# A new list-scheduled head, and weight blocks grouped over three and two PSUM banks, in an RMSNorm and QKV projection kernel

## The chip, the cores and the metric

The kernel runs on one core of one Trainium2 chip. The metric is the device time of one execution in microseconds (us). A kernel's time is the median of its runs. Single-core runs have no second die to be compared with, so a run counts as fast unless it is over 1.5% above the fastest run of the same kernel. The mean clock that the throttle granted to TensorE is recorded for each run, and it will matter here. In the profiles PE is TensorE's matmuls and PEld its weight loads; DVE, ACT and POOL are the vector, scalar and GpSimd engines; SP is the engine that issues the transfers. "The ring" or "the rings" is the queue of transfers that SP has issued and that the DMA engines work off.

## The reference

```python
def reference(x, gamma, w_qkv, eps):
    rms = np.sqrt(np.mean(x ** 2, axis=-1, keepdims=True) + eps)
    x_norm = x / rms * gamma
    return np.matmul(x_norm, w_qkv).astype(np.float32)
```

x is 8 × 1024 × 768 in float32, which makes 8192 rows. w_qkv is 768 × 2304. The kernel takes the rows in 64 tiles of 128. A tile needs six blocks of K (768 / 128) and five pieces of N (four of 512 columns and one of 256), so it takes 24 matmuls of full width and 6 of half width.

## The kernel before

Every tile of x is loaded, cast to bf16 and transposed to xT. The blocks of xT are the weights that TensorE loads, and w_b (w_qkv times gamma, in bf16) streams past them. The sum of a tile and a piece lies in one PSUM bank; `evac` scales it by 1/rms on DVE or ACT into `ot`, and a store brings it out.

```python
def load_x(t):
    X[t] = xin.tile([P, K], f32, name="x_t")
    nc.sync.dma_start(out=X[t], in_=xf[t * P:(t + 1) * P, :])
# load_w and store are nc.sync.dma_start too
def trans_dma(t):
    XT[t] = xTp.tile([P, KO, P], bf16, name="xT")
    nc.sync.dma_start_transpose(out=XT[t], in_=XB[t])

def mm(t, n0, kos):
    nl = min(NT, N - n0)
    for ko in kos:
        ...  # takes a PSUM bank on first use
        nc.tensor.matmul(out=PM[t, n0][:, :nl], lhsT=XT[t][:, ko, :],
                         rhs=w_b[:, ko, n0:n0 + nl], start=(b == 1), stop=(b == KO))
```

All loads, stores and DMA transposes are issued from SP, in one order. `at(time, ...)` puts an operation into a list, which is sorted by the planned time before anything is issued. The times only fix the order. An operation that has to wait holds up those behind it on its engine: in the trace of the changed kernel SP issued nothing from 11.89 to 20.02 us, in front of a transpose whose input came at 19.99, and a load that needed nothing from it was issued only after that, at 21.39.

The first six tiles are the head. They run while w_qkv is still arriving, by a list of planned operations, and there TensorE itself transposes all six tiles ("tr" and "cp"). The loads are all put first:

```python
ARRIVALS = "xxxwwwxwwwwwxxwww"            # order of the loads of x tiles and w pieces
HEAD_PLAN = [ (4.41, "trA", 0), ...
    (17.24, "tr", 4), ... (18.02, "cp", 4, "DVE"), (18.23, "tr", 5), ...
    (19.86, "mm", 4, 0, "012345"), ... (22.45, "mm", 5, 0, "012345"), ... ]
HEAD_END = 44.51

US = 6 * 0.2158 / 512
now, flip = HEAD_END, 0
for t in range(HEAD, MT):
    at(now - 15, load_x, t)
    at(now - 8.5, cast, t)
    at(now - 7.5, trans_dma, t)
    ...                                     # stat, recip
    for n0 in range(0, N, NT):
        at(now, mm, t, n0, range(KO))
        now += min(NT, N - n0) * US
        flip ^= 1
        evac_at(now + 0.2, t, n0, "DVE" if flip else "ACT", gap=1.2)   # and the store after it
```

Of the kernel before, what the change touches and what calls it, by code (L numbers as in the profile page):

```python
# [7 lines left out]



ARRIVALS = "xxxwwwxwwwwwxxwww"
PIECES = [(0, 1, 0, 512), (1, 2, 0, 512), (2, 3, 0, 512), (3, 4, 0, 512), (4, 5, 0, 512), (5, 6, 0, 512), (0, 3, 512, 512), (3, 6, 512, 512), (0, 6, 1024, 512), (0, 6, 1536, 512), (0, 6, 2048, 256)]

EARLY = 3


HEAD_PLAN = [
    (4.41, "trA", 0), (4.45, "stat", 0), (5.28, "trB", 0), (5.42, "cpA", 0, "DVE"),
    (5.71, "trA", 1), (5.85, "cpB", 0, "ACT"), (6.10, "recip", 0), (6.44, "stat", 2),
    (6.59, "trB", 1), (6.73, "cpA", 1, "DVE"), (6.80, "trA", 2), (7.11, "conv", 0, 0, "POOL"),  # L20
    (7.24, "trB", 2), (7.41, "cpB", 1, "DVE"), (7.77, "cpA", 2, "ACT"),
    (7.81, "conv", 1, 1, "DVE"), (8.02, "mm", 0, 0, "0"), (8.23, "mm", 1, 0, "0"),
    (8.29, "recip", 2), (8.39, "cpB", 2, "ACT"), (8.45, "conv", 2, 2, "DVE"),
    (8.45, "mm", 2, 0, "0"), (8.66, "mm", 0, 0, "1"), (8.75, "stat", 1), (8.88, "mm", 1, 0, "1"),
    (9.10, "mm", 2, 0, "1"), (9.31, "mm", 0, 0, "2"), (9.44, "cast", 3, "DVE"),
    (9.53, "mm", 1, 0, "2"), (9.74, "mm", 2, 0, "2"), (10.05, "tr", 3), (10.08, "stat", 3),
    (10.11, "conv", 3, 3, "DVE"), (10.59, "recip", 1), (10.65, "mm", 0, 0, "3"),
    (10.78, "conv", 4, 4, "DVE"), (10.87, "mm", 1, 0, "3"), (11.09, "mm", 2, 0, "3"),
    (11.26, "cp", 3, "DVE"), (11.32, "mm", 0, 0, "4"), (11.45, "conv", 5, 5, "ACT"),
    (11.54, "mm", 1, 0, "4"), (11.76, "mm", 2, 0, "4"), (11.82, "recip", 3),  # L30
    (11.97, "mm", 3, 0, "01234"), (13.05, "mm", 0, 0, "5"), (13.27, "mm", 1, 0, "5"),
    (13.47, "conv", 6, 0, "DVE"), (13.47, "conv", 6, 1, "ACT"), (13.47, "conv", 6, 2, "POOL"),
    (13.48, "mm", 2, 0, "5"), (13.70, "mm", 3, 0, "5"), (13.95, "evac", 2, 0, "DVE"),
    (14.01, "mm", 0, 512, "0"), (14.18, "evac", 0, 0, "ACT"), (14.22, "mm", 1, 512, "0"),
    (14.44, "mm", 0, 512, "12"), (14.70, "evac", 1, 0, "DVE"), (14.87, "evac", 3, 0, "ACT"),
    (14.87, "mm", 1, 512, "12"), (15.30, "mm", 2, 512, "012"), (15.48, "conv", 7, 4, "DVE"),
    (15.48, "conv", 7, 5, "POOL"), (15.95, "mm", 3, 512, "012"), (16.33, "conv", 7, 3, "POOL"),
    (16.47, "cast", 4, "DVE"), (16.47, "stat", 4), (16.60, "mm", 0, 512, "45"),
    (17.03, "mm", 1, 512, "4"), (17.24, "tr", 4), (17.47, "cast", 5, "DVE"),
    (17.58, "mm", 0, 512, "3"), (17.79, "mm", 1, 512, "35"), (17.80, "stat", 5),  # L40
    (18.02, "cp", 4, "DVE"), (18.23, "tr", 5), (18.56, "mm", 2, 512, "345"), (18.58, "recip", 4),
    (18.74, "evac", 1, 512, "DVE"), (19.13, "evac", 0, 512, "ACT"), (19.21, "mm", 3, 512, "345"),
    (19.49, "evac", 2, 512, "DVE"), (19.86, "mm", 4, 0, "012345"), (20.02, "evac", 3, 512, "ACT"),
    (20.24, "recip", 5), (20.40, "cp", 5, "DVE"), (21.15, "mm", 4, 512, "012345"),
    (21.49, "conv", 8, 2, "DVE"), (21.49, "conv", 8, 3, "ACT"), (21.97, "conv", 8, 0, "DVE"),
    (22.20, "conv", 8, 4, "ACT"), (22.45, "mm", 5, 0, "012345"), (22.45, "evac", 4, 0, "DVE"),
    (22.91, "evac", 4, 512, "ACT"), (23.60, "conv", 8, 1, "ACT"), (23.74, "mm", 5, 512, "012345"),
    (23.90, "evac", 5, 0, "DVE"), (24.31, "conv", 8, 5, "ACT"), (25.04, "mm", 0, 1024, "012345"),
    (25.20, "evac", 5, 512, "DVE"), (25.51, "conv", 9, 0, "POOL"), (25.51, "conv", 9, 1, "ACT"),
    (25.95, "conv", 9, 5, "DVE"), (26.33, "mm", 1, 1024, "012345"), (26.43, "conv", 9, 4, "DVE"),  # L50
    (26.49, "evac", 0, 1024, "ACT"), (26.91, "conv", 9, 2, "DVE"), (27.39, "conv", 9, 3, "DVE"),
    (27.63, "mm", 2, 1024, "012345"), (27.87, "evac", 1, 1024, "DVE"),
    (27.90, "conv", 10, 0, "POOL"), (27.90, "conv", 10, 2, "ACT"), (28.38, "conv", 10, 3, "ACT"),
    (28.62, "conv", 10, 5, "DVE"), (28.86, "conv", 10, 4, "ACT"), (28.92, "conv", 10, 1, "DVE"),
    (28.92, "mm", 3, 1024, "012345"), (29.22, "evac", 2, 1024, "DVE"),
    (30.22, "mm", 4, 1024, "012345"), (30.38, "evac", 3, 1024, "DVE"),
    (31.51, "mm", 5, 1024, "012345"), (31.67, "evac", 4, 1024, "DVE"),
    (32.81, "mm", 0, 1536, "012345"), (32.97, "evac", 5, 1024, "DVE"),
    (34.10, "mm", 1, 1536, "012345"), (34.26, "evac", 0, 1536, "DVE"),
    (35.39, "mm", 2, 1536, "012345"), (35.55, "evac", 1, 1536, "DVE"),  # L60
    (36.69, "mm", 3, 1536, "012345"), (36.85, "evac", 2, 1536, "DVE"),
    (37.98, "mm", 4, 1536, "012345"), (38.14, "evac", 3, 1536, "DVE"),
    (39.28, "mm", 5, 1536, "012345"), (39.44, "evac", 4, 1536, "DVE"),
    (40.57, "mm", 0, 2048, "012345"), (40.73, "evac", 5, 1536, "DVE"),
    (41.23, "mm", 1, 2048, "012345"), (41.39, "evac", 0, 2048, "ACT"),
    (41.88, "mm", 2, 2048, "012345"), (42.04, "evac", 1, 2048, "DVE"),
    (42.54, "mm", 3, 2048, "012345"), (42.70, "evac", 2, 2048, "DVE"),
    (43.19, "mm", 4, 2048, "012345"), (43.35, "evac", 3, 2048, "DVE"),
    (43.85, "mm", 5, 2048, "012345"), (44.01, "evac", 4, 2048, "DVE"),
    (44.67, "evac", 5, 2048, "DVE"),  # L70
]
HEAD_END = 44.51


@with_exitstack
def kernel(
# [8 lines left out]
    nc = tc.nc  # L85
    f32 = mybir.dt.float32
# [7 lines left out]
    Kw, N = w_qkv.shape  # L94
    assert K == Kw
    P = 128
    KO = K // P
    MT = M // P
    NT = 512
    HEAD = ARRIVALS.count("x")  # L100
    inv_k = 1.0 / float(K)
    PIECE_BUFS = {(k1 - k0, n): sum((q[1] - q[0], q[3]) == (k1 - k0, n) for q in PIECES)
                  for k0, k1, _, n in PIECES}

# [7 lines left out]
    xbp = ctx.enter_context(tc.tile_pool(name="xbp", bufs=4))  # L112
    xTp = ctx.enter_context(tc.tile_pool(name="xTp", bufs=HEAD + 3))
    outp = ctx.enter_context(tc.tile_pool(name="outp", bufs=7))
    psum = ctx.enter_context(tc.tile_pool(name="psum", bufs=8, space=bass.MemoryType.PSUM))
# [17 lines left out]
    w_b = singles.tile([P, KO, N], bf16)  # L133
    wv = w_qkv.rearrange("(ko p) n -> p ko n", p=P)

    X, XB, XT, RS, OUT, WF, PM, PT = {}, {}, {}, {}, {}, {}, {}, {}
# [5 lines left out]
    def load_w(c):  # L142
        k0, k1, n0, n = PIECES[c]
        WF[c] = wst.tile([P, k1 - k0, n], f32, name=f"w_f{k1 - k0}_{n}", bufs=PIECE_BUFS[k1 - k0, n])
        nc.sync.dma_start(out=WF[c], in_=wv[:, k0:k1, n0:n0 + n])  # L145

    def conv(c, ko, eng):
        k0, k1, n0, n = PIECES[c]
        o, i, g = w_b[:, ko, n0:n0 + n], WF[c][:, ko - k0, :], g_sb[:, ko:ko + 1]
# [60 lines left out]
# [3 lines that stand above are left out]
            if (t, n0) not in PM:  # L213
# [2 lines left out]
            nc.tensor.matmul(out=PM[t, n0][:, :nl], lhsT=XT[t][:, ko, :], rhs=w_b[:, ko, n0:n0 + nl],  # L216
                             start=(b == 1), stop=(b == KO))

    def part(n0):
        return max(i for i, (p0, _) in enumerate(PARTS) if p0 <= n0)  # L220

# [20 lines left out]
    def at(time, fn, *args):  # L242
        plan.append((time, len(plan), fn, args))
# [8 lines left out]
    def evac_at(time, t, n0, eng, gap):  # L252
        at(time, evac, t, n0, eng)
        h = part(n0)
        nl = min(NT, N - n0)
        left[t, h] = left.get((t, h), PARTS[h][1]) - nl
        if t == MT - 1:
            at(time + gap - 0.5, store, t, h, n0, nl)
        elif left[t, h] == 0:
            at(time + gap, store, t, h, *PARTS[h])  # L260
# [4 lines left out]
            nc.tensor.matmul(out=wps, lhsT=warm, rhs=warm, start=True, stop=True)  # L265


    nx = nw = 0
    for n, kind in enumerate(ARRIVALS):
        if kind == "x":  # L270
            at(0.1 * n - 9, load_x, nx)
            nx += 1
        else:
            at(0.1 * n - 9, load_w, nw)
            nw += 1
    at(0.0, idle, 30)
    ops = {"conv": conv, "cast": cast, "stat": stat, "recip": recip, "tr": tr, "cp": cp, "mm": mm}
    for time, op, *args in HEAD_PLAN:
# [14 lines left out]
    US = 6 * 0.2158 / 512  # L293
    now, flip = HEAD_END, 0
    for t in range(HEAD, MT):
        at(now - 15, load_x, t)
        at(now - 8.5, cast, t)
        at(now - 7.5, trans_dma, t)
        at(now - 5, stat, t)
        at(now - 3, recip, t)  # L300
        for n0 in range(0, N, NT):
            at(now, mm, t, n0, range(KO))
            now += min(NT, N - n0) * US
            flip ^= 1
            evac_at(now + 0.2, t, n0, "DVE" if flip else "ACT", gap=1.2)

    for _, _, fn, args in sorted(plan, key=lambda p: p[:2]):
        fn(*args)
# [35 lines left out]
```

## Time and profile before

| | before |
|---|---|
| time, median of 3 runs | 389.47 us (389.18 to 389.6) |
| span of the profiled run | 387.9 us |
| TensorE's share of the chain that ended last | 94% |
| first matmul of the product | 8.5 us |
| start of tile 6, the end of the head | 45.1 us |
| start of tile 7, and time of one tile from there on | 51.56 us, 5.835 us |
| granted TensorE clock | full in all slices |

The kernel is bound by TensorE; the prediction shows the lines and the sums. So there is little to gain, while a loss has no such limit.

### The profile page before, as it was taken

What the parts mean: (1) busy time and instruction counts of PE and PEld (TensorE: products, weight loads), DVE (VectorE), ACT (ScalarE), POOL (GpSimd) and SP (SyncE); (2) the same over time, 40 slices, a digit from 0 to 9 for tenths busy, and PEclk for the clock granted to TensorE, in tenths of its full rate; (3) what the DMA queues carried; (4) which work ended last, traced back from release to release, by engine and by line L of the source; (5) the groups of instructions that cost most, each with busy time, mean ns of one, the idle gap of its engine ahead of it and who ended that gap; (6) DMA issues with size and microseconds to landing.
All of it is one profiled execution on the core that took longest, in us unless ns stands there. A gap on an engine that the chain in (4) does not pass through costs nothing.

```text
span 387.9 us, 5500 instructions
## 1 busy us (share of the span) xinstructions
PE 379.5 (98%) x1953; PEld 194.3 (50%) x1992; DVE 159.1 (41%) x317; ACT 178.1 (46%) x359; POOL 5.9 (2%) x12
## 2 busy tenths in 40 slices
PE   7999999999999999999999999999999999999996
PEld 6444644554554554554554554554554554554553
DVE  3667634343433343433343433343334343334332
ACT  6652234544444544444534444534434535434532
POOL 1310000000000000000000000000000000000000
PEclk9999999999999999999999999999999999999999
DMA  7999999999999999999999999999999999999974
GB/s 272 392 384 358 308 369 284 397 301 274 333 311 305 279 326 295 290 330 300 276 346 288 302 317 280 318 311 304 287 318 301 297 318 303 287 325 292 292 264 189
DMA packets 87606, 119.51 MB, mean 308 GB/s; under 512 B 50710, under 2 KB 59676, under 8 KB 87580
## 3 DMA queue, kind: packets, MB, share of 16 engines
q1 hardware_dynamic: 87568, 119.17, 100.7%
q8 instruction: 15, 0.25, 0.3%
q14 instruction: 11, 0.09, 0.1%
q10 hardware_dynamic: 12, 0.00, 0.0%
HBM read 32.25 MB, written 75.50 MB: 278 GB/s over the span
## 4 chain that ended last, share of the span: by engine, by line
PE 94%; DMA 3%; SPq 1%; issue 1%; DVE 0%; ACT 0%
PE pm L216 94%; DMA w_f<-in_w_qkv_dram 2%; DMA xT<-xb 2%; SPq L140 0%; SPq L145 0%; PE pm L183 0%; DVE w_b L151 0%; ACT ot L232 0%; DVE ot L230 0%
## 5 line engine op out<-in xcount | busy, mean ns | idle before, releaser
L216 PE MATMUL pm<-w_b,xT 128*128 128x512 bf16 (+1 forms) x1881 | 372.4, 357 | 3.0 <-DMA xT<-xb 0.4
L216 PEld LDWEIGHTS <-xT 128*128 128x128 bf16 x1920 | 187.6, 98 | 186.6 <-issue 0.8
L230 DVE TENSOR_SCALAR ot<-pm,rstd 128x512 f32<-128x512 f32 (+1 forms) x168 | 116.7, 696 | 210.3 <-PE pm L216 210.3
L232 ACT ACTIVATE ot<-pm,rstd 128x512 f32<-128x512 f32 (+1 forms) x152 | 97.9, 645 | 187.0 <-PE pm L216 141.7
L170 ACT ACTIVATE sq<-x_t 128x768 bf16<-128x768 f32 x64 | 53.4, 834 | 10.2 <-DMA x_t<-in_x_dram 10.2
L159 DVE CAST xb<-x_t 128x768 bf16<-128x768 f32 x61 | 33.2, 545 | 4.1 <-DMA x_t<-in_x_dram 4.0
L172 ACT ACTIVATE rms<-ssq,eps_sb 128x1 f32<-128x1 f32 x64 | 18.8, 294 | 2.1
L170 ACT ACTIVATION_READ_ACCUMULATOR sq<-x_t 128x1 f32 x64 | 12.2, 191 | 0.0
L177 DVE RECIPROCAL rstd<-rms 128x1 f32<-128x1 f32 x64 | 9.8, 153 | 0.0
L151 DVE TENSOR_SCALAR w_b<-w_f,g_sb 128x512 bf16<-128x512 f32 (+1 forms) x14 | 6.5, 494 | 6.1 <-DMA w_f<-in_w_qkv_dram 6.0
L153 ACT ACTIVATE w_b<-w_f,g_sb 128x512 bf16<-128x512 f32 (+1 forms) x10 | 6.1, 651 | 5.7 <-DMA w_f<-in_w_qkv_dram 5.7
L155 POOL TENSOR_SCALAR w_b<-w_f,g_sb 128x512 bf16<-128x512 f32 (+1 forms) x6 | 5.2, 864 | 23.5 <-DMA w_f<-in_w_qkv_dram 23.5
L265 PE MATMUL pm<-warm 128*128 128x128 bf16 x35 | 3.8, 300 | 1.0 <-DVE eps_sb L124 1.0
L265 PEld LDWEIGHTS <-warm 128*128 128x128 bf16 x35 | 3.5, 142 | 1.0 <-DVE eps_sb L124 1.0
L197 PE MATMUL pm<-ident_f,x_t 128*128 128x128 f32 x18 | 2.8, 292 | 0.8 <-DMA x_t<-in_x_dram 0.8
L197 PEld LDWEIGHTS pm<-ident_f,x_t 128*128 128x128 f32 x18 | 2.2, 155 | 1.1 <-DMA x_t<-in_x_dram 1.0
L127 ACT ACT_TABLE_LOAD x1 | 1.3, 1283 | 1.3 <-PEq L325 1.3
L159 DVE CAST xT<-pm 128x512 bf16<-128x512 f32 (+1 forms) x3 | 1.7, 596 | 0.0
L159 DVE COPY xT<-pm 128x768 bf16<-128x768 bf16 x3 | 1.6, 547 | 0.0
L248 DVE COPY g_sb<-pm 128x6 f32<-128x6 f32 x1 | 0.2, 165 | 3.6 <-PE pm L247 3.6
L183 PEld LDWEIGHTS <-xb 128*128 128x128 bf16 x18 | 1.2, 98 | 0.9 <-DVE xb L159 0.6
L183 PE MATMUL pm<-ident,xb 128*128 128x128 bf16 x18 | 1.5, 220 | 0.0
(13 smaller groups left out, 3.1 us busy)
## 6 DMA issues: line engine op xcount, KB each, us to landing
out_dram<-ot SPq DMA_DIRECT2D x126, 512.0 KB, 4.0
x_t<-in_x_dram SPq DMA_DIRECT2D x64, 384.0 KB, 4.3
out_dram<-ot SPq DMA_DIRECT2D x64, 128.0 KB, 3.2
w_f<-in_w_qkv_dram SPq DMA_DIRECT2D x2, 1536.0 KB, 13.3
w_f<-in_w_qkv_dram SPq DMA_DIRECT2D x3, 768.0 KB, 8.5
w_f<-in_w_qkv_dram SPq DMA_DIRECT2D x6, 256.0 KB, 5.8
out_dram<-ot SPq DMA_DIRECT2D x4, 256.0 KB, 2.0
xT<-xb SPq DMA_TRANSPOSE x58, 4.4
```

The costliest lines, as they stand in the source:

```text
L151: nc.vector.tensor_scalar(out=o, in0=i, scalar1=g, scalar2=None, op0=mult)
L153: nc.scalar.activation(out=o, in_=i, func=AF.Copy, scale=g, bias=0.0)
L155: nc.gpsimd.tensor_scalar(out=o, in0=i, scalar1=g, scalar2=1.0, op0=mult, op1=mult)
L159: nc.vector.tensor_copy(out=out, in_=in_)
L170: nc.scalar.activation(out=sq, in_=X[t], func=AF.Square, accum_out=ssq)
L172: nc.scalar.activation(out=rms, in_=ssq, func=AF.Sqrt, scale=inv_k, bias=eps_sb)
L177: nc.vector.reciprocal(out=r, in_=RS[t])
L197: nc.tensor.transpose(out=PT[t, h][:, ko - k0, :], in_=X[t][:, ko * P:(ko + 1) * P], identity=ident_f)
L216: nc.tensor.matmul(out=PM[t, n0][:, :nl], lhsT=XT[t][:, ko, :], rhs=w_b[:, ko, n0:n0 + nl], start=(b == 1), stop=(b == KO))
L230: nc.vector.tensor_scalar(out=o, in0=pm[:, :nl], scalar1=RS[t], scalar2=None, op0=mult)
L232: nc.scalar.activation(out=o, in_=pm[:, :nl], func=AF.Copy, scale=RS[t], bias=0.0)
L265: nc.tensor.matmul(out=wps, lhsT=warm, rhs=warm, start=True, stop=True)
```

## The change

It has two parts. The loop after the head takes the pieces of N in a group of three and a group of two, goes through the six weight blocks once for each group, and marks all but the first matmul of a block as needing no weight load. In the head, a new list moves the transposes of tiles 4 and 5 from TensorE to the DMA, cuts the weight pieces smaller, and puts the last three of them (w11, w12 and w13) and the tiles x6 and x7 behind those transposes.

```diff
-ARRIVALS = "xxxwwwxwwwwwxxwww"
-PIECES = [(0, 1, 0, 512), ... , (0, 6, 2048, 256)]
+PIECES = [ ... (0, 2, 512, 512), (2, 4, 512, 512), (4, 6, 512, 512), (0, 3, 1024, 512), (3, 6,
+          1024, 512), (0, 3, 1536, 512), (3, 6, 1536, 512), (0, 6, 2048, 256)]
+LOADS = [
+    (-9.00, "x", 0), ... (-8.86, "x", 4),
+    (-8.85, "w", 10), (-8.84, "x", 5), (18.73, "t", 4), (18.74, "w", 11), (22.11, "t", 5),
+    (22.12, "w", 12), (22.13, "w", 13), (22.14, "x", 6), (22.15, "x", 7),
+]
 HEAD_PLAN = [ ...                      # all times and the order are new; no "tr" or "cp" of 4 and 5
-HEAD_END = 44.51
+HEAD_END = 43.73
...
+    def mm_shared(t, n0s):
+        for n0 in n0s:
+            PM[t, n0] = psum.tile([P, NT], f32, name="pm")
+        for ko in range(KO):
+            for n0 in n0s:
+                ...
+                if n0 == n0s[0]:
+                    m = nc.tensor.matmul(out=o, lhsT=l, rhs=r, start=(ko == 0), stop=(ko == KO - 1))
+                    lhs = m.ins.ins[1]
+                else:
+                    nc.tensor.add_instruction(mybir.InstMatmult( ...
+                        ldweights=False, ins=[nc.tensor.lower_ap(r), lhs], ...))
...
-    nx = nw = 0
-    for n, kind in enumerate(ARRIVALS):
-        ...
+    for time, kind, n in LOADS:
+        at(time, {"x": load_x, "w": load_w, "t": trans_dma}[kind], n)
...
     for t in range(HEAD, MT):
-        at(now - 15, load_x, t)
+        if ("x", t) not in {q[1:] for q in LOADS}:
+            at(now - 15, load_x, t)
...
-        for n0 in range(0, N, NT):
-            at(now, mm, t, n0, range(KO))
-            ...
+        n0s = list(range(0, N, NT))
+        groups = [[n0] for n0 in n0s] if t == MT - 1 else [n0s[:3], n0s[3:]]
+        for g in groups:
+            at(now, mm_shared, t, g)
+            now += sum(min(NT, N - n0) for n0 in g) * US
+            for j, n0 in enumerate(g):
+                flip ^= 1
+                evac_at(now + 0.2 + 0.35 * j, t, n0, "DVE" if flip else "ACT", gap=1.2)
```

## The prediction

The prediction reckons with 2.5 ns per matmul, which can be worked out from the trace of before. From 70 to 370 us matmuls of 512 columns start 215.83 ns apart in the mean and those of 256 columns 109.17 ns, so 2 × 109.17 - 215.83 = 2.5 ns of a matmul do not go with its columns. The weight loads of 98 ns run beside the matmuls there: one matmul starts at 100.198 us and a load at 100.199. The pool for the sums has eight tiles in PSUM, and the kernel issues everything on SP in one order.

> **What bounds the kernel now.** I read the page first (engine shares, the slices, the chain's shares, the costliest groups), then the tile view of xT, then the chain and the timelines piece by piece.
>
> ```profile
> span 387.9 us, 5500 instructions
> PE 379.5 (98%) x1953; PEld 194.3 (50%) x1992; DVE 159.1 (41%) x317; ACT 178.1 (46%) x359; POOL 5.9 (2%) x12
> PEclk9999999999999999999999999999999999999999
> GB/s 272 392 384 358 308 369 284 397 301 274 333 311 305 279 326 295 290 330 300 276 346 288 302 317 280 318 311 304 287 318 301 297 318 303 287 325 292 292 264 189
> ...
> PE 94%; DMA 3%; SPq 1%; issue 1%; DVE 0%; ACT 0%
> ...
> L216 PE MATMUL pm<-w_b,xT 128*128 128x512 bf16 (+1 forms) x1881 | 372.4, 357 | 3.0 <-DMA xT<-xb 0.4
> L216 PEld LDWEIGHTS <-xT 128*128 128x128 bf16 x1920 | 187.6, 98 | 186.6 <-issue 0.8
> ```
>
> TensorE is the bound: 94% of the chain is its matmuls, at full clock, and they idle 3.0 us in all. The weight loads are counted busy for 187.6 us, but on their own row beside the matmuls. What matters is whether a load delays the next matmul, and the timeline of TensorE in the steady stretch answers it:
>
> ```profile
> 99.98 3.62 PE L216 MATMUL pm<-w_b,xT 128*128 128x512 bf16 x16
> ```
>
> Sixteen matmuls of 512 columns span 3.62 us; the last is shown as 0.379 us long, so 15 starts lie in 3.24 us: 0.216 us each. [...]every one of these matmuls has a 98 ns load of its own. The load is already hidden.
>
> The tile view of xT gives the ends of the stream, and the timeline of the weight loads gives the only wait outside the head:
>
> ```profile
> L216 PE MATMUL pm<-w_b,xT x1881: 272/379/390, 8.5 to 384.1; 128*128 128x512 bf16 x147, 128*128 128x256 bf16 x42
> ...
> DMA to landing us min/median/max: 3.2/4.4/6.9
> ```
>
> ```profile
> 51.56 10.48 PEld L216 LDWEIGHTS <-xT 128*128 128x128 bf16 x53 [0.72 <-DMA xT<-xb]
> ```
>
> Tile 7 starts at 51.56. From there to about 384.17 (the last start plus 0.11) 57 tiles run, 332.6 us, 5.835 us per tile of 24 full and 6 half-width matmuls. All 64 tiles are 373.4 us of streaming. The stretch from 8.5 to 384.17 is 375.7, so only 2.3 us of it is not streaming: 0.7 for PE transposes of tiles 4 and 5, 0.3 for tile 3's, 0.6 for the wait before tile 7 (0.72 less one half-width matmul), the rest small waits for converted weights before 15 us. Outside lie 8.5 us before the first real matmul and 3.7 us after the last.
>
> Two chain pieces show the transposes' cost on the path, and one the wait:
>
> ```profile
> 17.99 0.34 PE pm L183 x6
> ...
> 19.01 0.34 PE pm L183 x6
> ...
> 45.48 6.04 DMA xT<-xb
> ```
>
> [...]every matmul here has its own load, so nothing in it says whether the 2.5 ns belongs to the matmul or to the change of weights. [...]groups of three and two need five per tile. [...]all loads, stores and transposes here are issued from SP. [...]the timeline of SP before tile 7's transpose is
>
> ```profile
> 40.43 2.26 SPq L236 DMA_DIRECT2D out_dram<-ot  x3
> 42.78 1.05 SPq L140 DMA_DIRECT2D x_t<-in_x_dram  x1
> 43.92 1.46 SPq L236 DMA_DIRECT2D out_dram<-ot  x2
> 45.48 1.39 SPq L206 DMA_TRANSPOSE xT<-xb  x1
> ```
>
> Five stores and a load lay ahead of it, and it took 6.04 us against a median of 4.4: that made the 0.6 us wait.
>
> **The change, part by part.**
>
> Part one, shared weights. For 57 tiles (6 to 62) 30 loads become 12, so 57 × 18 = 1026 loads of 98 ns vanish, 100 us of load-row time, all beside other work. On the path only the 2.5 ns can go, and only if it belongs to the load: 1026 × 2.5 ns = 2.6 us. [...]I give the saving 35 in 100, so about -0.9 as expectation. The last load of each pair group (98 ns) still hides under a half-width matmul (109 ns), as it does now.
>
> PSUM: the group of three takes 24/6 × 0.97 = 3.88 us, the group of two 1.94. The first bank of a group of two is the eighth allocated before it, in the three of the previous tile's group; there is more than 3.8 us to empty it, against 0.7 us per eviction on either engine. DVE and ACT are 41% and 46% busy, and their work is unchanged. No wait.
>
> Part two, the head. Removed: twelve PE transposes, 2 × 0.34 = 0.7 us on the path, which is nearly all of what the plan's own end promises (43.73 for 44.51). Moved: tiles 4 and 5 are transposed by DMA; three late weight pieces are issued after those transposes; x6 and x7 are loaded early, so tile 7's 0.6 us wait should go.
>
> The new order puts transfers in front of transposes. I follow the ring. Through x5 the queue holds 6 × 384 KB of x and 6 × 256 + 3 × 512 + 2 × 768 KB of weights, 7.08 MB. The slices of 9.70 us moved 2.64 and 3.80 MB, then 0.384 MB/us: reached at 19.4 + 0.64/0.384 = 21.1 us. A check of the method on the kernel before: its x5 stood at 5.50 MB, reached at 9.7 + 2.86/0.392 = 17.0, and its cast began at 18.03, so landing costs 1 us more.
>
> ```profile
> 18.03 0.56 DVE L159 CAST xb<-x_t 128x768 bf16<-128x768 f32 x1 [0.44 <-DMA x_t<-in_x_dram]
> ```
>
> After the change x4 (5.90 MB) lands near 19.0, its cast ends at 19.6, and its transpose goes into the ring behind w10 and x5; with 1 to 2 us of its own it lands near 23. Tile 4 is wanted at 24.26 by the plan, plus about 0.6, by which the kernel before ran behind its plan (tile 6 began at 51.56 - 0.6 - 5.835 = 45.1 for 44.51). That fits. Tile 5 does not: by the plan's order w11 (0.79 MB) and the first stores of tiles 0 to 3 (4 × 512 KB = 2.10 MB) are issued between the two transposes. From 22.6: w11 to 24.6; the stores, at the rate that the windows view shows where stores alone ran,
>
> ```profile
> 44.00:47.00 3.00, 2.95 (x20) 1.88 (x20) 1.83 (x4) 0.00 (x0) 0.00 (x0) 1.00 1.03 422
> ```
>
> take 5.0 us, to 29.6; the transpose lands about 31. TensorE wants tile 5 at 28.15 + 0.6 = 28.75. The estimate is a wait of 2.3 us, between 1 and 4.
>
> After that w12 lands near 33 and w13 near 35; their matmuls come at 36 and 40 plus the delay, so they fit. The six second stores are now released every 0.65 us by plan (1.3 before), 3.1 MB in front of tile 7's transpose: I expect 0.4 us of wait there, between 0 and 1.
>
> Sum: -0.7 (transposes) - 0.6 (old wait) + 2.3 (tile 5) + 0.4 (tile 7) = +1.4; with the -0.9 for shared weights +0.5. 389.47 + 0.5 = 390.0 us.
>
> **Rivals.** One: the 2.5 ns is the price of changing weights. For it: the trace has no matmul without a load to contradict it. [...]It would make 388.3 with my head (+1.4 - 2.6). Two: the transposes are not held up, because stores leave gaps that they use or the 1 to 2 us are shorter; for it: steady transposes land in 4.4 us with stores about, and from 22.7 that is 27.1, in time. Then the head gains 1.3: 388.2, or 385.6 with rival one. Three: the ring holds up more than I think (transposes that stall behind others, w11 to w13 late as well): tile 4 also waits and tile 7 again, 393. Four: matmuls that keep their weights are slower, or lose the pull-ahead of the next load and show 98 ns per group and row: 57 × 12 × 0.1 = 68 us slower. Against it: loads are issued in order just before the matmul that needs them, as now. Under 4 in 100.
>
> **Range and chances.** The path can't shrink by more than 2.3 + 2.6 us plus a little at the start, so 2% (7.8 us) faster is all but excluded; slower by 7.8 needs rival four. Rivals one and two set the low end (386.8), rival three the high end (392.4).
>
> **What would show it.** Weight loads fall to about 960 and their busy time to about 94 us. The starts of matmuls in the steady stretch stay 0.2158 apart (parts: 5.835 us per tile); 5.79 would prove rival one. The chain shows a wait for DMA xT<-xb at tile 5 around 28 to 31 us, with DMA busy on 4096-byte store packets before it; if there is none, my ring argument is wrong. Tile 6 starts at 46 to 47.5 (before 45.1). A tile period over 5.9, or evictions on the chain, would make the prediction wrong altogether.

## The result, and the profile after

Ratios here are the mean time of one kernel's fast runs over that of the kernel before in the same rounds, so they are not quite the ratio of the medians that are quoted beside them.

| | before, same rounds | after |
|---|---|---|
| median | 389.54 us (4 runs) | 395.38 us (4 runs, 393.44 to 396.94) |
| ratio, 95% interval | | 1.0148 (1.0102 to 1.0194) |
| start of tile 6 | 45.1 us | 49.89 us |
| start of tile 7 | 51.56 us | 56.63 us |
| time of one tile from there on | 5.835 us | 5.835 us |

The change is 1.5% slower, which is outside the predicted range of 386.8 to 392.4 us. The four runs differ more than those of before, and the granted clock follows them:

| run of after, us | 395.19 (profiled) | 393.44 | 396.94 | 395.58 |
|---|---|---|---|---|
| span, us | 393.1 | 391.3 | 394.8 | 393.4 |
| mean granted clock | 0.996 | 1.000 | 0.990 | 0.996 |
| span × clock, us | 391.5 | 391.3 | 390.9 | 391.8 |

Without the throttle all four spans would be about 391.4 us. So about 3.5 us are lost in every run (391.4 against before's 387.9), and 0 to 4 us more differ from run to run.

The page of the changed kernel has these lines where the prediction shows those of before. In the groups the columns are line, engine, operation, tiles, shapes, count, busy us, mean ns, and the idle time ahead of them with what ended it.

```profile
span 393.1 us, 5526 instructions
PE 383.0 (97%) x1980; PEld 194.1 (49%) x1980; DVE 159.8 (41%) x312; ACT 174.5 (44%) x357; POOL 7.9 (2%) x17
PEclk9998999999999999999999999999999999999999
...
PE 90%; DMA 8%; SPq 1%; DVE 0%; issue 0%; ACT 0%
...
L241 PE MATMUL pm<-w_b,xT 128*128 128x512 bf16 (+1 forms) x714 | 246.8, 378 | 0.7 <-DMA xT<-xb 0.7
...
L244 PEld LDWEIGHTS <-xT 128*128 128x128 bf16 x1026 | 100.4, 98 | 84.6
...
L229 PE MATMUL pm<-w_b,xT 128*128 128x512 bf16 (+1 forms) x180 | 37.4, 368 | 4.2 <-DMA xT<-xb 3.5
```

Three things stand here. First, line 244 is the matmul marked as needing no load, and yet 1,026 weight loads of 98 ns bear its name. With 714 of line 241 and 180 of line 229 there are 1,920 loads of xT, exactly as before. Sharing did not happen at all. The loads stand in the built program: an experiment below takes the repeated ones out of it, and 894 of 1,920 are left in its trace. Second, the idle time ahead of the head's matmuls (line 229) is 4.2 us, of which a transpose ended 3.5. Third, the fourth slice of the clock shows an 8.

The timeline of TensorE shows where the first wait lies (start, length, engine, line, operation and count; the idle time ahead is in brackets).

```profile
27.19 2.11 PE L229 MATMUL pm<-w_b,xT 128*128 128x512 bf16 x9
32.76 4.95 PE L229 MATMUL pm<-w_b,xT 128*128 128x512 bf16 x15 [3.47 <-DMA xT<-xb]
```

At 32.76 tile 5 begins. The last matmul ahead of it is drawn 0.38 us long, while a matmul takes 0.22 from start to start, so the delay is 3.47 + 0.38 - 0.22 = 3.63 us. The same working gives 0.90 us for tile 7, whose transpose ended a wait of 0.74 us after a half-width matmul: 0.74 + 0.27 - 0.11. The chain that ended last has both, and both times it goes through a transpose (start, length, what):

```profile
25.32 7.40 DMA xT<-xb
...
32.76 17.31 PE pm L229 x90
...
51.09 5.49 DMA xT<-xb
```

The windows view of the stretch around the first wait shows what came behind it (from and to, length, busy time of PE, PEld, DVE, ACT and POOL with counts, granted clock, DMA share, GB/s).

```profile
29.00:32.70 3.70, 0.30 (x2) 0.00 (x0) 0.75 (x1) 0.00 (x0) 0.00 (x0) 0.97 1.10 341
32.70:35.80 3.10, 3.04 (x8) 1.09 (x9) 0.26 (x1) 0.00 (x0) 0.96 (x2) 0.50 1.06 369
35.80:49.80 14.00, 14.00 (x84) 8.02 (x83) 7.77 (x15) 5.09 (x11) 2.48 (x5) 1.00 0.88 310
```

For 3.1 us after the wait TensorE ran at half clock, and then it ran at full clock again. Eight matmuls took 3.27 us instead of 1.73, so 1.55 us are lost. That is the whole throttle of this run: 0.4% of 393 us.

Why the transpose came so late is to be seen four to twelve us earlier. The timeline of SP, with nothing issued between 12 and 20 us:

```profile
20.02 1.32 SPq L219 DMA_TRANSPOSE xT<-xb  x1
21.39 0.57 SPq L158 DMA_DIRECT2D w_f<-in_w_qkv_dram  x1
22.05 3.17 SPq L268 DMA_DIRECT2D out_dram<-ot  x4
25.32 2.23 SPq L219 DMA_TRANSPOSE xT<-xb  x1
```

SP stood in front of tile 4's transpose until the cast of x4 ended at 19.99, and w11, which needed nothing from it, stood behind. Then came the four stores, and then tile 5's transpose. That is the order which the prediction had followed. What it had not seen is how little the rings moved meanwhile, here in the windows view of before and then of after:

```profile
20.00:24.00 4.00, 4.00 (x20) 1.83 (x19) 2.09 (x6) 1.53 (x4) 0.00 (x0) 1.00 1.05 387
```

```profile
20.00:24.00 4.00, 3.96 (x20) 1.70 (x18) 2.56 (x6) 2.82 (x8) 0.00 (x0) 1.00 0.91 175
```

Before moved 387 GB/s here, after moved 175. The mean busy share is nearly the same (1.05 and 0.91), but it hides two things. From 20.5 to 21.5 us and from 23 to 24 us it is 0.56 and 0.64, so there the DMA engines partly lacked work. From 21.5 to 22 us it is 2.29 (packets overlap) with only 212 GB/s, so there the packets were slow: the DMA view of these four us has 822 of 1,019 packets under 512 bytes. The experiment with w11 first, below, gives an estimate of what each is worth. The shortfall is (387 - 175) × 4 = 0.85 MB, which at 0.39 MB/us is 2.2 us of transfer pushed back.

### The profile page after: what moved, and what is told of

Its sections match the earlier page's. It is cut to its first block, busy times and chain, and to the rows that moved or that the text cites. A ratio compares the mean times of both kernels' runs of the same rounds, so it can differ in the third digit from the quotient of the medians.

```text
span 393.1 us, 5526 instructions
## 1 busy us (share of the span) xinstructions
PE 383.0 (97%) x1980; PEld 194.1 (49%) x1980; DVE 159.8 (41%) x312; ACT 174.5 (44%) x357; POOL 7.9 (2%) x17
## 4 chain that ended last, share of the span: by engine, by line
PE 90%; DMA 8%; SPq 1%; DVE 0%; issue 0%; ACT 0%
PE pm L244 46%; PE pm L241 38%; PE pm L229 5%; DMA xT<-xb 3%; DMA w_f<-in_w_qkv_dram 3%; DMA x_t<-in_x_dram 2%; SPq L158 0%; SPq L153 0%; DVE w_b L164 0%; DVE ot L262 0%; ACT ot L264 0%; SPq L268 0%; DVE rstd L190 0%; SPq L219 0%
## 5 line engine op out<-in xcount | busy, mean ns | idle before, releaser
L244 PE MATMUL pm<-w_b,xT 128*128 128x512 bf16 (+1 forms) x1026 | 296.6, 344 | 0.0
L241 PE MATMUL pm<-w_b,xT 128*128 128x512 bf16 (+1 forms) x714 | 246.8, 378 | 0.7 <-DMA xT<-xb 0.7
L264 ACT ACTIVATE ot<-pm,rstd 128x512 f32<-128x512 f32 (+1 forms) x154 | 96.4, 646 | 194.4 <-PE pm L244 93.8
L262 DVE TENSOR_SCALAR ot<-pm,rstd 128x512 f32<-128x512 f32 (+1 forms) x166 | 112.4, 693 | 145.7 <-PE pm L241 72.0
L229 PE MATMUL pm<-w_b,xT 128*128 128x512 bf16 (+1 forms) x180 | 37.4, 368 | 4.2 <-DMA xT<-xb 3.5
L172 DVE CAST xb<-x_t 128x768 bf16<-128x768 f32 x61 | 34.0, 558 | 8.9 <-DMA x_t<-in_x_dram 8.7
L166 ACT ACTIVATE w_b<-w_f,g_sb 128x512 bf16<-128x512 f32 (+1 forms) x6 | 3.8, 648 | 13.2 <-DMA w_f<-in_w_qkv_dram 13.2
L168 POOL TENSOR_SCALAR w_b<-w_f,g_sb 128x512 bf16<-128x512 f32 (+1 forms) x11 | 7.2, 663 | 30.1 <-DMA w_f<-in_w_qkv_dram 22.7
```

What stands on the lines that cost most here:

```text
L168: nc.gpsimd.tensor_scalar(out=o, in0=i, scalar1=g, scalar2=1.0, op0=mult, op1=mult)
L172: nc.vector.tensor_copy(out=out, in_=in_)
L241: m = nc.tensor.matmul(out=o, lhsT=l, rhs=r, start=(ko == 0), stop=(ko == KO - 1))
L244: nc.tensor.add_instruction(mybir.InstMatmult(name=nc.get_next_instruction_name(), engine=m.ins.engine, start_tensor_calc=(ko == 0), stop_ ...
L262: nc.vector.tensor_scalar(out=o, in0=pm[:, :nl], scalar1=RS[t], scalar2=None, op0=mult)
L264: nc.scalar.activation(out=o, in_=pm[:, :nl], func=AF.Copy, scale=RS[t], bias=0.0)
```

## The experiments

All twelve kernels gave correct results. They ran in three batches, each on a chip of its own; each batch had its own runs of the kernel before (medians 389.86, 390.16 and 389.98 us), and every kernel is compared with those of its batch. "Loss" is the kernel's median minus that of before in the same rounds. For the change itself it is 395.38 - 389.54 = 5.84 us. Differences between the losses of two batches are less sharp than those within one.

### Which half of the change costs, the grouping or the head?

**Old head, grouped loop.** The kernel before with `mm_shared` and the grouped loop.

```diff
+    def mm_shared(t, n0s): ...            # as in the change
-        for n0 in range(0, N, NT): ...
+        groups = [[n0] for n0 in n0s] if t == MT - 1 else [n0s[:3], n0s[3:]]
+        ...
```

> The head of before with the grouped loop of the change. The built program still has a weight load ahead of every matmul, so theory A (the grouping changes nothing but the order) expects the time of before, 389.5 us within 0.5, 1920 loads of xT, and a tile period of 5.835 us. Rival B (the groups of three and two cost something by themselves, through evictions or the clock) expects 391 us or more. Rival C (some loads are saved on the chip) expects 387 us.

Measured: 389.76 us (13 runs), ratio 0.9999 (0.9991 to 1.0007). Grouping by itself changes nothing. The tile view of xT shows once more that the loads are there:

```profile
L231 PEld LDWEIGHTS <-xT x1026: 97/98/99, 45.2 to 378.0; 128*128 128x128 bf16 x171
```

**New head, plain loop.** The changed kernel with the loop of before.

```diff
-        groups = ...
+        for n0 in range(0, N, NT):
+            at(now, mm, t, n0, range(KO))
+            ...
```

> The head of the change with the plain loop of before: the other half of the change. Theory A expects the whole loss here: 393.4 to 397 us, the wait for tile 5's transpose of 3 to 4 us near 29 us, and the same spread from run to run. Rival B expects less than half of the loss, under 392.

Measured: 397.47 us (4 runs, 396.08 to 398.41), ratio 1.0194 (1.0172 to 1.0216), a loss of 7.6 us. This profiled run too has half clock behind the wait for tile 5, and that wait is longer, 4.25 us against 3.63. The time lies half a us above the expected range. The whole loss is in the head. In the profiled run the plain loop even makes it larger: tile 7 waits 0.99 us here and tile 8 waits 0.78. The intervals of the two kernels overlap, so that part is not shown by the times.

### Would really sharing the weights have gained anything?

**Loads dropped.** Old head and grouped loop, and the repeated loads are taken out of the built program, with their waits moved to the matmul that follows. The edit is given in words:

```diff
+   # in the built program, for the PE instructions in order:
+   #   a Ldweights of xT with the operand of the Ldweights before it is left out;
+   #   what it waited for is put on the next Matmult
```

It sets the case that the 2.5 ns belong to the matmul (389.7 us, 5.835 us per tile) against the case that they belong to the change of weights.

> As e1_old_head_grouped, but the repeated weight loads are taken out of the built program, so that 894 loads of xT stay of 1920: what the change meant to do, with the head of before. [...]the time is that of e1, 389.7 within 0.3, and a tile takes 5.835 us. If they belong to the change of weights, 1026 times 2.5 ns go: 387.1 within 0.4, and a tile takes 5.79 us. If matmuls that keep their weights are slower or expose the next load: over 392.

Measured: 389.48 us (22 runs), ratio 0.9986 (0.9978 to 0.9995). Only line 231 of this kernel, the shared matmuls, has lost its loads. Its tile view of xT:

```profile
L231 PE MATMUL pm<-w_b,xT x1003: 272/379/379, 46.0 to 378.6; 128*128 128x512 bf16 x111, 128*128 128x256 bf16 x57
L228 PEld LDWEIGHTS <-xT x714: 96/98/98, 45.6 to 384.4; 128*128 128x128 bf16 x179
L228 PE MATMUL pm<-w_b,xT x702: 272/379/390, 45.8 to 384.5; 128*128 128x512 bf16 x174, 128*128 128x256 bf16 x2
```

Line 231 has no row of loads any more, so 714 + 180 = 894 loads are left of 1,920. Tile 7 begins at 51.98 in this run, and the last matmul at 384.5: (384.5 + 0.11 - 51.98) / 57 = 5.835 us per tile, to the nanosecond that of before. So the 2.5 ns belong to the matmul and not to the change of weights. The timing shows 0.14% less than before, in a batch whose runs of before were the highest of the three; the profile has no place where this would have been gained, and the last experiment looks at it again.

### What makes tile 5 wait, and what is the wait worth?

**First stores after x7.** In the changed kernel the first stores of tiles 0 to 3 go behind the transpose of tile 5 and what follows it.

```diff
-            at(time + gap, store, t, h, *PARTS[h])
+            at(22.16 if t < 4 and h == 0 else time + gap, store, t, h, *PARTS[h])
```

> The changed kernel, but the first stores of tiles 0 to 3 are issued after the transpose of tile 5, w12, w13, x6 and x7 instead of before them. Theory (the transpose of tile 5 waits in the ring behind w11 and 2.1 MB of stores): it lands near 27 us, the wait at tile 5 (3.6 us) and the half clock after it (1.7 us in the profiled run) go, the spread of the runs shrinks below 0.5 us, and the time is 388.5 to 390.5. Rival (the transpose is slow by itself, or its issue from SP is what comes late): a wait of over 2 us stays, 392 us or more.

Measured: 393.86 us (5 runs), ratio 1.0099 (1.0082 to 1.0116), a loss of 4.0 us. The wait for tile 5 is gone, so it needed the stores in front of that transpose. But the loss is mostly still there: a wait of 3.0 us stands at tile 7, and the clock is again 0.996 in four runs of five. The two queues of TensorE at that place:

```profile
53.99 0.10 PEld L241 LDWEIGHTS <-xT 128*128 128x128 bf16 x1 [3.25 <-DMA xT<-xb]
```

```profile
53.99 0.50 PE L241 MATMUL pm<-w_b,xT 128*128 128x512 bf16 x1 [2.87 <-DVE ot L262]
```

The same wait has two names. I first believed the second line and the chain that ended last, which went through DVE: DVE stood 6.2 us in front of the cast of x8, and the eviction that frees TensorE stood behind it. The next experiment rests on that reading, and it was wrong. The weight load comes before the matmul, and its wait of 3.25 us ended with the transpose. Tile 7's transpose, issued at 47.49, landed at 53.95; DVE's eviction ended 20 ns later and took the name.

**The same, with x8 and x9 loaded early.**

```diff
-    (22.14, "x", 6), (22.15, "x", 7),
+    (22.14, "x", 6), (22.15, "x", 7), (22.152, "x", 8), (22.154, "x", 9),
```

> As e3_stores_after, with x8 and x9 loaded right after x6 and x7. Theory (the wait left in e3 is the cast of tile 8 on VectorE, which waits for x8 and holds up the evictions behind it): the wait near 51 us and the half clock go, no wait over 0.3 us after tile 5, mean clock 1.000 in all runs, 388.3 to 389.3 us, that is slightly faster than before. Rival (there is more in the ring than can be moved in that time): the wait moves on to another transfer, 391 or more.

Measured: 395.57 us (5 runs), ratio 1.0136 (1.0109 to 1.0163), a loss of 5.4 us. The theory fell. Two more loads now lay ahead of the stores, and the wait split into 2.26 us at tile 6 and 1.55 us at tile 7. The chain of this kernel shows both transposes; the first is the slowest of the study:

```profile
38.26 10.12 DMA xT<-xb
...
48.45 9.03 DMA xT<-xb
```

**This with the loads dropped.** The kernel above with the repeated weight loads taken out, as the change had intended.

> e6_stores_after_x8 with the repeated loads taken out as in e7_loads_dropped: the sum of the two. If e6 gains 0.9 us and e7 nothing, 388.3 to 389.3; if e7 gains 2.6, 386 to 387.

Measured: 396.10 us (4 runs), ratio 1.0145 (1.0119 to 1.0171), a loss of 5.9 us. A wait of 3.8 us stands at tile 7, with half clock behind it. Nothing is gained over the kernel above, so neither idea of mine mends this head.

**TensorE kept busy in the wait.** The changed kernel with sixty small matmuls on a constant tile, into a PSUM bank that nothing reads, just ahead of tile 5.

```diff
+    at(28.14, idle, 60)
```

> The changed kernel with 60 dummy matmuls of 128 columns (some 3.3 us) placed in TensorE's order just before tile 5, that is in the wait. Theory (a wait of 3.6 us lets the clock fall to half for a while, and how long differs from run to run): no window at half clock after tile 5 starts, mean clock 1.000 in every run, 393.4 us within 0.5, and the spread of 3.5 us goes. Rival (the eight slow matmuls after the wait are slow for want of data or bank space): they stay slow and the time stays at 395 or rises.

Measured: 393.61 us (5 runs), ratio 1.0106 (1.009 to 1.0122), a loss of 3.75 us against 5.84. The sixty small matmuls took 3.51 us. The wait is the same, but the window behind it now has full clock, and the mean clocks are 1.0, 1.0, 0.998, 1.0 and 0.999:

```profile
32.70:35.80 3.10, 2.93 (x17) 1.34 (x15) 0.75 (x1) 0.00 (x0) 0.68 (x2) 1.00 1.03 359
```

So half clock was a cost of its own, some 2 us in the median, and it hangs on TensorE's idling. The spread is down from 3.5 to 1.6 us. The 393.6 us agree with the 391.4 + 2 us that the table of spans gives for runs without throttle (a run is about 2 us longer than its span: 395.19 against 393.1 us in the profiled run).

How long the wait is does not decide it alone. The packed trace keeps the moments at which the granted clock changed (the views show only the mean). In the profiled run of the change, full clock lasted 27.31 us, then half clock 3.413 us (32.49 to 35.91), then full clock 358.40 us; in that of before, full clock lasted 382.29 us. These are 8, 1, 105 and 112 times 3.413 us, so the clock is looked at here in steps of that length. In the step ahead of the half clock of the change TensorE idled 3.20 us. The windows view over such steps, first of the kernel with x8 and x9 early (a wait of 2.26 us, all of it in one step), then of the kernel with unread transposes below (a wait of 3.07 us, split over two):

```profile
45.34:48.75 3.41, 1.31 (x12) 0.85 (x10) 1.73 (x5) 0.00 (x0) 0.00 (x0) 1.00 0.49 172
48.75:52.16 3.41, 3.19 (x9) 1.21 (x9) 0.00 (x0) 0.00 (x0) 0.00 (x0) 0.50 1.03 419
```

```profile
49.87:53.28 3.41, 1.89 (x12) 0.97 (x10) 1.09 (x2) 2.01 (x5) 0.00 (x0) 1.00 0.98 340
53.28:56.69 3.41, 2.02 (x10) 0.96 (x11) 1.24 (x4) 0.24 (x1) 0.00 (x0) 1.00 1.09 268
```

The first kernel idled 2.10 us (3.41 - 1.31) in one step, and the next ran at half clock. The second idled 1.52 and 1.39 us in its two steps, and the clock stayed full. With w11 first, below, it also stayed full, after a wait of 1.86 us. So of the waits of 2.26 and 3.07 us the longer one left the clock full. That it matters how a wait falls on the steps is a reading of these few cases, which would fit that runs of one kernel differ; no run tested it. One stretch does not fit: with the loads dropped from the kernel with x8 and x9 early, half clock went on for a second step after one with 1.33 us of idling (the mean clock of that run is 0.991, that of the change with one step 0.996).

### Is it the backlog as such, or the two transposes?

**Tiles 4 and 5 transposed by TensorE, in the new head.**

```diff
-    ... (18.73, "t", 4), ... (22.11, "t", 5),
+    (20.30, "tr", 4), (20.46, "cp", 4, "DVE"), ... (23.60, "tr", 5), ... (23.64, "cp", 5, "DVE"),
```

> The changed kernel with tiles 4 and 5 transposed on TensorE again (0.7 us on the path), every load and store in the changed kernel's order. Theory (the store backlog is the cause and only moves): no wait at tile 5, but TensorE arrives 4 us earlier at the end of the head, where x8 stands in the ring behind the second stores, so a wait of 2 to 4 us shows near tile 7 or 8 and the time is 392 to 394.5. Rival (the two DMA transposes alone are the loss): no wait anywhere, 389 to 390.

Measured: 390.36 us (21 runs), ratio 1.0016 (1.0001 to 1.003), a loss of 0.2 us. I had expected that the backlog would only move to a later transpose; that fell, and the rival held. The same weights, tiles of x and stores are transferred, and no wait of size is left (0.15 us at tile 7 in the profiled run). Five of the 21 runs have a mean clock of 0.991 to 0.996 and take 391.4 to 394.1 us; they have no trace, so where that half clock lies stays open. The window that the change had starved:

```profile
20.00:24.00 4.00, 3.80 (x22) 1.83 (x22) 3.02 (x8) 2.67 (x7) 0.00 (x0) 1.00 1.04 403
```

**The same, with the two DMA transposes added back into tiles that nobody reads.** No matmul waits for them now, so all that they can do is take time of SP and of the rings.

```diff
+    def trans_unread(t):
+        unread = singles.tile([P, KO, P], bf16, name=f"unread{t}")
+        nc.sync.dma_start_transpose(out=unread, in_=XB[t])
+    # LOADS has (18.73, "t", 4) and (22.11, "t", 5) again, as trans_unread
```

> e5_pe_transposes (tiles 4 and 5 transposed on TensorE) with the two DMA transposes put back in their places, into tiles that nothing reads: the ring's share of the loss without the dependence of tiles 4 and 5. Theory (the two transposes cost the rings 2 us or more each, and the backlog then comes out at the next transfer that is needed): no wait at tile 5, GB/s between 20 and 24 us under 250, and a wait of 1 to 3 us at tile 6, 7 or 8; 391.5 to 394 us. Rival (only the dependence costs): no wait, 390.4 within 0.5 as e5.

Measured: 393.12 us (6 runs), ratio 1.0086 (1.0057 to 1.0116), a loss of 3.1 us against 0.2 without them (two of the six runs, 394.59 and 396.23 us, have a mean clock under 0.996). The same window falls to 151 GB/s, and the wait stands at tile 7 (3.07 us by the working above; the load queue shows it as 3.29):

```profile
20.00:24.00 4.00, 3.81 (x22) 1.82 (x22) 3.04 (x8) 3.09 (x8) 0.00 (x0) 1.00 0.75 151
```

```profile
54.66 0.10 PEld L245 LDWEIGHTS <-xT 128*128 128x128 bf16 x1 [3.29 <-DMA xT<-xb]
```

This shows the cause. Two transposes at this place cost about 2.9 us (3.14 - 0.20), even though nothing waits for them, because the transfers that are ordered behind them come late. The loads, the stores and the pieces of the weights in the new order cost next to nothing without these transposes. What this run does not part is the two ways in which a transpose delays the rest: SP stands in front of it until its cast has ended, and the transfer itself is slow. The next one parts them in part.

**w11 issued ahead of tile 4's transpose.** One line of the changed kernel: the piece that had stood behind the cast of x4 goes first.

```diff
-    (18.73, "t", 4), (18.74, "w", 11), (22.11, "t", 5),
+    (18.72, "w", 11), (18.73, "t", 4), (22.11, "t", 5),
```

> The changed kernel with w11 issued before the transpose of tile 4 instead of after it: one line of the order. In the changed kernel the DMA engines moved only 175 GB/s between 20 and 24 us (387 before). Theory A (the rings ran dry because SP stood at the transpose, with w11 behind it): 20 to 24 us shows over 300 GB/s, tile 5's transpose lands 1.5 to 2 us earlier, and the wait at tile 5 falls from 3.6 to 1.5 to 2.5 us. Theory B (a transpose itself takes 2 us or so of the rings, wherever it stands): the slow stretch moves to 22 to 26 us, the transpose of tile 5 lands as late as before, and a wait of over 1 us appears at tile 4 too; 394 to 398 us.

Measured: 392.06 us (4 runs, 391.92 to 392.14), ratio 1.0047 (1.0033 to 1.0062), a loss of 2.1 us instead of 5.8. The window moves 307 GB/s and the wait for tile 5 is 1.70 + 0.38 - 0.22 = 1.86 us:

```profile
20.00:24.00 4.00, 3.46 (x16) 1.51 (x16) 2.15 (x7) 2.37 (x7) 0.00 (x0) 1.00 1.30 307
```

```profile
31.10 1.25 PE L229 MATMUL pm<-w_b,xT 128*128 128x512 bf16 x5 [1.70 <-DMA xT<-xb]
```

Theory A held. With the shorter wait TensorE's clock stays full (0.999 to 1.000 in the four runs), and the runs lie within 0.22 us of each other. So here an independent transfer ahead of the transpose filled the rings while SP stood (307 GB/s against 175). Theory B is right in a part: from 20 to 28 us the windows view has 380 GB/s in the kernel before, 275 in the change and 341 here, so the shortfall goes from 0.84 MB to 0.31 MB, or from 2.2 to 0.8 us at 0.38 MB/us. By this estimate 1.4 us was w11 held back behind a transpose that could not be issued yet, and 0.8 us is left with the transposes in place. From 23 to 24 us, while tile 4's transpose was in the rings and other transfers were queued, they moved 100 GB/s, and in the kernel before 381. In the rest of the wait four stores, 2.10 MB, still lie ahead of tile 5's transpose.

### Without the wait at tile 7

**Before, with tile 7's operations earlier.** The kernel before waits 0.6 us at tile 7. Its load, cast and transpose are moved up by 3 to 4 us.

```diff
-        at(now - 15, load_x, t)
-        at(now - 8.5, cast, t)
-        at(now - 7.5, trans_dma, t)
+        soon = t == HEAD + 1
+        at(now - (19.3 if soon else 15), load_x, t)
+        at(now - (11.5 if soon else 8.5), cast, t)
+        at(now - (10.8 if soon else 7.5), trans_dma, t)
```

> The kernel before with x7 loaded, cast and transposed some 3 to 4 us earlier, so that its transpose is issued ahead of the stores it waited behind. Theory: the 0.6 us wait at tile 7 goes and nothing comes in its place: 0.5 us faster than before, 389.3 for 389.9. Rival (it only moves to tile 8): no difference.

Measured: 389.69 us (13 runs), ratio 0.9993 (0.9984 to 1.0002). The wait is gone from the profile, but the gain of 0.3 us lies within the interval.

**This with the grouped loop and the loads dropped.**

> e11_before_tile7 with the grouped loop and the repeated weight loads dropped as in e7_loads_dropped. If the small gain seen in e7 (0.1%) is real and not chance, 0.3 to 0.5 us under e11; if not, the same as e11 within 0.2 us.

Measured: 389.57 us (20 runs), ratio 0.999 (0.9983 to 0.9996). Its page:

```profile
span 387.0 us, 4476 instructions
PE 379.5 (98%) x1953; PEld 94.1 (24%) x966; DVE 162.8 (42%) x317; ACT 175.1 (45%) x359; POOL 5.9 (2%) x12
```

It has half the weight loads and is 0.1% faster than before, with an interval that only just leaves out 1. By the losses above (5.84 and -0.41 us, from different batches) it is 1.6% faster than the change. Against the kernel just above, 0.12 us are left for 1,026 dropped loads, which these intervals cannot tell from nothing. Whether dropping them gains a few tenths of a us somewhere stays open; the tile period says that it gains nothing in the loop.

### All runs together

| kernel | loss, us | longest waits of TensorE in the profiled run, us | half clock in it, ahead of the end |
|---|---|---|---|
| the change | 5.84 | 3.63 (tile 5), 0.90 (tile 7) | yes |
| old head, grouped loop | -0.10 | 0.6 (tile 7), as before | no |
| new head, plain loop | 7.61 | 4.25 (tile 5), 0.99 (tile 7), 0.78 (tile 8) | yes |
| stores after x7 | 4.00 | 3.0 (tile 7) | yes |
| stores after, x8 and x9 early | 5.41 | 2.26 (tile 6), 1.55 (tile 7) | yes, and once near 8 us |
| this, loads dropped | 5.94 | 3.8 (tile 7) | yes |
| kept warm | 3.75 | filled | no |
| TensorE transposes | 0.20 | 0.15 (tile 7) | no |
| this, with unread transposes | 3.14 | 3.07 (tile 7) | no |
| w11 first | 2.08 | 1.86 (tile 5), 0.89 (tile 7) | no |
| old head, loads dropped | -0.68 | 0.4 (tile 7) | no |
| old head, tile 7 earlier | -0.29 | none of size | no |
| this, loads dropped | -0.41 | none of size | no |

## Why the prediction was wrong

The terms of its sum, and what the runs showed in their place:

| term of the sum | predicted, us | measured, us |
|---|---|---|
| TensorE transposes of tiles 4 and 5 removed | -0.7 | -0.7 |
| old wait at tile 7 removed | -0.6 | -0.6 |
| shared weights (expectation) | -0.9 | 0 |
| tile 5 waits for its transpose | +2.3 | +3.63 |
| tile 7 waits for its transpose | +0.4 | +0.90 |
| half clock behind the wait | not in the sum | +1.55 in the profiled run, 0 to 4 in all |
| sum | +0.5 | +4.8 |

The spans of the two profiled runs differ by 393.1 - 387.9 = 5.2 us. The 0.4 us left were not taken apart; the chain shows one wait for w10, near 22 us. The -0.7 and -0.6 are read from what is gone from the trace, not timed by themselves.

**What bounds the kernel: right.** TensorE and the head's transfers decide. The tile period is 5.835 us in both kernels, no eviction came onto the path, and PSUM did not wait, as the prediction said.

**Shared weights: wrong in the premise, right in the worth.** "1026 loads of 98 ns vanish" did not happen: the trace has 1,920 loads of xT as before, 1,026 of them at the marked matmuls. The prediction leaned to no gain and gave the other reading 35 in 100; the trace that it had did not decide between them. The kernel with the loads really dropped shows 5.835 us with 894 loads as with 1,920. The -0.9 was an expectation for nothing. Rival one fell, and rival four did not come either.

**The order of the ring: right.** Tile 4 came in time without a wait, tile 5 waited for its transpose behind w11 and four stores, and w12 and w13 fitted. Rival two, that the transposes would not be held up, fell.

**The size of the wait at tile 5: too small, and this is the step that failed first.** The prediction took the ring to run at 0.384 MB/us all the time and let tile 4's transpose take "1 to 2 us of its own", so that it would be done by 22.6 and w11 by 24.6. In the trace that transpose ran from 20.02 to 23.4, and over 21 to 24 us the rings moved 131 GB/s or 0.39 MB, half of it the transpose itself (0.20 MB). From 24.0 to 32.7 us the windows moved 381 × 5.0 + 341 × 3.7 = 3.17 MB, and w11, the four stores and the transpose are 0.79 + 2.10 + 0.20 = 3.09 MB. By this working little of w11 had been moved at 24.0, where the prediction had 1.4 of its 2.0 us behind it. Tile 5's transpose landed at 32.7 instead of 31, 1.7 us late; TensorE wanted it at 29.13 instead of 28.75, which takes 0.4 back. That gives 2.3 + 1.7 - 0.4 = 3.6 us. The runs confirm this cause: without these two transposes the loss is 0.2 us, with two that nobody reads it is 3.1, and with w11 ahead of the first it is 2.1. What the prediction had not counted is above all that w11 was issued only after the transpose, when the ring had run low (1.4 us by the estimate above). The wait lay within the stated 1 to 4, but the sum used its middle. At tile 7 the same mechanism gave 0.90 instead of 0.4.

**Half clock: missing.** The prediction had treated a wait as costing its own length. After 3.6 us of idling TensorE ran at half clock for 3.1 us. The prediction does not ask what a wait does to the clock. Its range went to 4 us of wait, but the upper end holds no cost of this kind. Keeping TensorE busy in the wait took 2.1 us off the loss, which shows it.

**The range.** Its high end came from rival three, "the ring holds up more than I think", which stood at 393 in the prediction's own text and was cut to 392.4 in the range. That rival was the nearest, though tile 4 did not wait, and 1.55 us of half clock came on top. The low end, 386.8, is none of the figures that the prediction worked out for rivals one and two (388.3 and 388.2, or 385.6 together). Rival four, the only way the prediction saw to over 2% slower, did not come.

## What to carry to other kernels

A DMA transpose in a ring that also carries loads and stores delayed what was ordered behind it here, even where nobody waited for the transpose: the loss was 3.14 us with two unread transposes and 0.20 us without them. Where such a ring is the bottleneck, leave small transposes to TensorE (a loss of 0.20 instead of 5.84 us here), or issue all that is independent ahead of them, so that the queue does not stand in front of a cast (2.08 instead of 5.84 us). When a change makes TensorE wait, add the stretch at half clock that may follow: of the six profiled runs here with an unfilled wait of 2.26 us or more, five have it, and in the change it was 3.41 us long and cost 1.55 us. And look into the trace whether an instruction that was to be saved has really gone.
